# The scale of the first quarter's x goes out to memory and back by GpSimd's queue

## The chip, the cores and the metric

The kernel runs on one core of a Trainium2 chip. A core has a matrix engine (TensorE, PE in the profile), a vector engine (VectorE, DVE), a scalar engine (ScalarE, ACT), GpSimd (POOL) and a queue engine (SyncE, SP), and 16 DMA engines that move data between the chip's memory and the core's. Each engine works through a list of instructions in order and waits at semaphores. The metric is device time in microseconds (us), the median of several runs.

## The reference

The kernel computes one layer of a hybrid decoder on a sequence of 2048 tokens of width 1024. What matters here is how the layer begins, and one part at its end:

```python
hn = rms_norm(h, pre_mix_norm[i])                       # h * rsqrt(mean(h*h) + EPS) * weight
proj = jnp.einsum('btd,dc->btc', hn, w_in[i])           # one projection for all mixers
...
g_dec = -jnp.exp(gdn_a_log[i]) * jax.nn.softplus(a_gdn + gdn_dt_bias[i])
...                                                     # DeltaNet and HGRN2 mixers, output projection, MLP
e = rms_norm(jnp.einsum('bte,ed->btd', p[i], w_ple_proj[i]), ple_norm[i])
gate = jax.nn.sigmoid(jnp.einsum('btd,de->bte', h, w_ple_gate[i]))
h = h + e * gate
```

The first line needs one number for each token, the scale rsqrt(mean(h*h) + EPS). The embedding e depends on p alone, so the kernel can compute it at any time.

## The kernel before, in words

The tokens are worked on in four quarters of 512 (NQ = 4, QT = 512), and all large tiles hold features on the 128 partitions and tokens along the row. Every 32-bit matmul is made of three matmuls of a high and a low part, so each operand tile is first split: ScalarE writes the rounded part (L160), VectorE subtracts it from the original (L161). These two lines serve all weights and inputs.

The kernel starts with a prologue (L349 to L394). It loads the embedding inputs (praw, raw_plea), x with tokens on the partitions (xs, four tokens a partition), x with features on the partitions (xraw) and constants, and computes the embedding tiles (q, d) of the first two quarters while x is made ready.

- The scale: ScalarE squares xs and sums along the row (L375), VectorE adds EPS (L376), GpSimd raises to the power -1/2 (L156, 128x4 numbers). The result ss stands four to a partition, but the tiles of x need it along the row and on every partition. So `spread` stores it to memory (L230, tensor rd_x, 2 KB) and `spread_load` loads it back with each partition reading the whole row (L235, tile rsb_x, 256 KB). VectorE then scales the eight tiles of xraw (L202), and each is split to xt.
- An embedding tile: six matmuls into one of two PSUM banks (L187, tile mme), then ScalarE copies it out (L297, tile e), squares it (L223, tile sq_e, of which there is one, or L220 for the first of a quarter), VectorE adds the square up (L224), and the copy is stored (L299, ed<-e). The square frees the bank for the next tile but one. Six copies e can be in flight.

After the prologue come the projections (from L1009 on): for each of 33 weight blocks of a quarter, 24 matmuls (L1021), first the block of decays (mm_ab), then those of the heads. The loads of the weights (L446), their splits and the stores of the split weights (L176, cache) are requested two or three blocks ahead; the weights of the first two blocks (raw_ab, and raw for the next) are requested at the start of this part. The decays' numbers run through ScalarE and VectorE (L460 to L470), and a short group of matmuls (L480, ps_gb) waits for them in TensorE's order.

The order on TensorE is fixed as the program is traced. On SP the requests of the prologue keep their order among themselves, and so do those of the projections, but the two sequences are merged. This merge, and the order on ScalarE, VectorE and GpSimd, is chosen by a scheduler when the kernel is built, by its own idea of when each input will be there. Once built, the order of each engine is fixed.

The functions that the edit touches:

Of the kernel before, what the change touches and what calls it, by code (L numbers as in the profile page):

```python
# [20 lines left out]
P = 128  # L21
# [3 lines left out]
QT = 512  # L25
NQ = T // QT
NC = QT // P
# [57 lines left out]
def trunk(ctx, tc, x, xT, pT, vecs, w_in, w_ab, gdn_a_log, gdn_dt_bias, w_out, w_up, w_down,  # L85
          w_ple, w_gate, consts, out):
    nc = tc.nc
    V, S, G, PE = nc.vector, nc.scalar, nc.gpsimd, nc.tensor
# [32 lines left out]
    def col(r):  # L121
        return cols[:, r : r + 1]
# [7 lines left out]
    def vectors():  # L130

        ps = bank("ps_rows", pp)
        PE.transpose(ps[:, :N_ROWS], rows, ident[:N_ROWS, :N_ROWS])
        V.tensor_copy(cols, ps[:, :N_ROWS])
        V.tensor_scalar(ple_w, cols[:, R_PLE : R_PLE + KD], 0.5, None, ALU.mult)
        V.tensor_tensor(lb, lg, lg, ALU.subtract)
        S.activation(lb, lb, AF.Exp)
        V.reciprocal(lb1, lb)
        V.tensor_tensor(lb, lb, lb1, ALU.mult)
        V.tensor_tensor(lb, lb, lb, ALU.subtract)  # L140
        V.tensor_scalar(ha, lb, -0.5, 0.5, ALU.mult, ALU.add)
        V.tensor_scalar(hna, ha, -1.0, None, ALU.mult)
        V.tensor_tensor(hb, lb, ha, ALU.add)
        S.activation(nexpa, dec[:, 0:1], AF.Exp)
        V.tensor_scalar(nexpa, nexpa, -1.0, None, ALU.mult)
# [9 lines left out]
    def rsqrt(v):  # L155
        G.tensor_tensor(v, v, mhalf, ALU.pow)  # L156
# [39 lines left out]
    def operand(pool, src, name, scale=None, rsb=None, raw=None, stage=None):  # L196

        if raw is None:
            raw = stage.tile([P, QT], F32, tag="ld", name=f"raw_{name}", bufs=2)
            nc.sync.dma_start(raw, src)  # L200
        if scale is not None:
            V.scalar_tensor_tensor(raw, raw, scale, rsb, ALU.mult, ALU.mult)  # L202
        t = pool.tile([P, 2, QT], F32R, tag="ring", name=name)
        split(t, V, raw)
        return t
# [18 lines left out]
            eng.tensor_tensor(acc, acc, sq, ALU.add)  # L224
        return acc

    def spread(m, name):

        rd = dr.tile([1, QT], F32, name=f"rd_{name}")
        nc.sync.dma_start(rd.rearrange("o (p n) -> (o p) n", n=NC), m)  # L230
        return rd

    def spread_load(rd, name, pool=None, tag="rsb", bufs=2):
        rsb = (pool or st).tile([P, QT], F32, tag=tag, name=f"rsb_{name}", bufs=bufs)
        nc.sync.dma_start(rsb, rd.broadcast_to([P, QT]))  # L235
        return rsb

    def row_norm(acc, scale, eps, name):
# [6 lines left out]
    def tok(q):  # L245
        return slice(q * QT, (q + 1) * QT)
# [30 lines left out]
    def stage_ple(i, name):  # L277

        raw = wp.tile([P, KD, P], F32, tag="raw", name=f"raw_{name}", bufs=2)
        nc.sync.dma_start(raw.rearrange("p (d k) n -> p d k n", k=2),  # L280
                          w_ple[4 * i : 4 * i + 4].rearrange("d p k n -> p d k n"))

        def ready(eng):
            w = wp.tile([P, 2, KD, P], F32R, tag="whl", name=f"w_{name}")
            for half in range(2):
                sl = slice(half * KD // 2, (half + 1) * KD // 2)
                split(w[:, :, sl], eng, raw[:, sl])
            return w

        return ready  # L290

    def embed_tile(q, d, w, pt, accs, pool, bufs):

        ps = bank(f"mme_{q}_{d}")
        project(ps, w[:, :, 2 * (d % 4) : 2 * (d % 4) + 2], pt)
        e = pool.tile([P, QT], F32, tag="ld", name=f"e{q}_{d}", bufs=bufs)
        S.activation(e, ps, AF.Copy)  # L297
        accs[q] = squares(accs[q], ps, d, f"e{q}")
        return lambda: nc.sync.dma_start(ed[q][d], e)  # L299
# [4 lines left out]
    x_r, xts, accs = {}, {0: []}, {0: None, 1: None}  # L304
# [44 lines left out]
    with ExitStack() as ectx:  # L349
        es = ectx.enter_context(tc.tile_pool(name="es", bufs=1))  # L350
        with tc.manual_schedule(engines={mybir.EngineType.SP}):
            ple0 = stage_ple(0, "plea0")
            praw = [es.tile([P, 2, QT], F32, name=f"praw{q}") for q in range(2)]
            nc.sync.dma_start(praw[0], pT[:, tok(0)].rearrange("(k p) t -> p k t", p=P))
            rows4 = x[tok(0), :].rearrange("(p c) d -> p c d", c=NC)
            xs = es.tile([P, NC, D], F32, name="xs")
            for c in range(0, NC, 2):
                nc.sync.dma_start(xs[:, c : c + 2], rows4[:, c : c + 2])
            nc.sync.dma_start(ident, consts[:, C_IDENT])
            nc.sync.dma_start(rows, vecs)  # L360
            nc.sync.dma_start(dec[:, 0:1], gdn_a_log.rearrange("o h -> h o"))
            nc.sync.dma_start(dec[:, 1:2], gdn_dt_bias.rearrange("o h -> h o"))
            nc.sync.dma_start(praw[1], pT[:, tok(1)].rearrange("(k p) t -> p k t", p=P))
            ple1 = stage_ple(1, "plea1")
            xraw = es.tile([P, KD, QT], F32, name="xraw")
            for k in range(0, KD, 2):
                nc.sync.dma_start(xraw[:, k : k + 2],
                                  xT[k * P : (k + 2) * P, tok(0)].rearrange("(k p) t -> p k t", p=P))
            nc.sync.dma_start(cst[:, C_NEG:], consts[:, C_NEG:])

            ple = [ple0(V), None]
            pts = [[operand(ra, None, f"pT{q}_{k}", raw=praw[q][:, k]) for k in range(2)] for q in range(1)]
            ss = sm.tile([P, NC], F32, tag="ss", name="ss_x0")
            for c in range(NC):
                S.activation(xs[:, c], xs[:, c], AF.Square, accum_out=ss[:, c : c + 1])  # L375
            V.tensor_scalar(ss, ss, 1.0 / D, EPS, ALU.mult, ALU.add)  # L376
            rsqrt(ss)
            stores = []
            for d in range(4):
                stores.append(embed_tile(0, d, ple[0], pts[0], accs, es, 6))  # L380
                if d == 1:
                    vectors()
            pts.append([operand(ra, None, f"pT1_{k}", raw=praw[1][:, k]) for k in range(2)])
            ple[1] = ple1(V)
            x_r[0] = spread(ss, "x0")
            rsb = spread_load(x_r[0], "x0")
            for d, q in [(d, 1) for d in range(4)] + [(d, q) for d in range(4, KD) for q in range(2)]:
                stores.append(embed_tile(q, d, ple[d // 4], pts[q], accs, es, 6))
                stores.pop(0)()
                if len(xts[0]) < KD:  # L390
                    k = len(xts[0])
                    xts[0].append(operand(ra, None, f"xt0_{k}", col(R_PREMIX + k), rsb, raw=xraw[:, k]))
            for f in stores:
                f()  # L394


    with mixers as mctx:
# [23 lines left out]
        def x_scale(q):  # L421
            ss2 = sm.tile([P, 2, NC], F32, tag="ss2", name=f"ss2_x{q}")
            rows4 = x[tok(q), :].rearrange("(p c) d -> p c d", c=NC)
            halves, loaded = [(c, a) for c in range(NC) for a in range(2)], []
            for i in range(len(halves) + 1):
                if i < len(halves):
                    c, a = halves[i]
                    t = m2.tile([P, QT], F32, tag="ld", name=f"xs{q}_{c}_{a}", bufs=2)
                    nc.sync.dma_start(t, rows4[:, c, a * QT : (a + 1) * QT])
                    loaded.append(t)  # L430
                if i:
                    c, a = halves[i - 1]
                    t = loaded.pop(0)
                    S.activation(t, t, AF.Square, accum_out=ss2[:, a, c : c + 1])
                yield
            ss = sm.tile([P, NC], F32, tag="ss", name=f"ss_x{q}")
            V.tensor_tensor(ss, ss2[:, 0, :], ss2[:, 1, :], ALU.add)
            V.tensor_scalar(ss, ss, 1.0 / D, EPS, ALU.mult, ALU.add)
            rsqrt(ss)
            yield  # L440
            x_r[q] = spread(ss, f"x{q}")
# [492 lines left out]
        def load_x(q):  # L934

            rsb = spread_load(x_r[q], f"x{q}", m2, "rsx", 1)
            raws = {}

# [737 lines left out]
    rsb = {q: spread_load(ple_r[q], f"pg{q}", None, "acc", 3) for q in (0, 1)}  # L1676
    es, puts = {(q, 0): embedded(q, 0, rsb[q]) for q in (0, 1)}, []
    for half in range(2):
# [4 lines left out]
        for d in range(KD):  # L1683
# [4 lines left out]
            if d + 1 == KD and half == 0:  # L1688
                rsb = {q: spread_load(ple_r[q], f"pg{q}", None, "acc", 3) for q in (2, 3)}
# [65 lines left out]
```

## Time and profile before

| | us |
|---|---|
| median of 3 runs | 2751.11 |
| lowest and highest | 2746.49, 2752.93 |
| the profiled execution | 2749.54 |
| its span in the profile | 2747.7 |

| engine | busy, share of the span |
|---|---|
| TensorE matmuls | 97% |
| VectorE | 74% |
| ScalarE | 54% |
| GpSimd | 4% |

In a row of the timeline stand the start, the duration, the engine, the line, the operation, the tiles it writes and reads, their shapes, and in brackets how long the engine had stood idle before it and what ended this. SPq is SP's queue at the issue of a DMA. A row of the chain of waits has start, duration and what the time went to.

### The profile page before, as it was taken

The page shows a single profiled execution, that of the slowest core. Times are in us where ns is not written, and L with a number is a line of the kernel's source. Part 1 is how long each engine was busy: PE and PEld are TensorE (multiplying, and loading weights), DVE is VectorE, ACT ScalarE, POOL GpSimd, SP SyncE. Part 2 cuts the span into 40 slices and gives each one's busy share as a digit, 9 for nine tenths or more (in the row PEclk, how much of TensorE's full clock was granted, in tenths as well). Part 3 has the DMA queues.
Part 4 walks back from the last instruction along what each step waited for, and adds up shares of the span by engine and source line. Part 5 has one row for each costly group of instructions (what it writes and reads, how often), then busy time and mean ns, then how long its engine had stood idle before and what let it go on. Part 6 is the DMA issues. An engine that isn't in the chain of part 4 may idle for free.

```text
span 2747.7 us, 38450 instructions
## 1 busy us (share of the span) xinstructions
PE 2663.1 (97%) x12745; PEld 2214.6 (81%) x12745; DVE 2044.8 (74%) x4244; ACT 1472.7 (54%) x2944; POOL 104.1 (4%) x104
## 2 busy tenths in 40 slices
PE   7999999999999999899899999999999999999999
PEld 5788788878888888777688888888888888888887
DVE  6788877777777777677798867867787765567776
ACT  6665555455546444666555645555455545465421
POOL 0000000000000000000000000001000000001000
PEclk9999999999999999999999999999999999999999
DMA  7776776666766665787466547667463446677664
GB/s 264 258 251 218 233 249 233 218 213 229 247 207 207 218 212 156 253 303 247 163 228 208 192 160 254 205 212 232 161 225 136 165 154 217 192 253 238 222 210 135
DMA packets 268742, 589.24 MB, mean 214 GB/s; under 512 B 55658, under 2 KB 60232, under 8 KB 249344
## 3 DMA queue, kind: packets, MB, share of 16 engines
q1 hardware_dynamic: 268544, 586.79, 64.4%
q8 instruction: 101, 1.65, 0.3%
q14 instruction: 97, 0.79, 0.1%
HBM read 419.75 MB, written 166.92 MB: 214 GB/s over the span
## 4 chain that ended last, share of the span: by engine, by line
PE 58%; DVE 9%; DMA 6%; issue 5%; ACT 2%; POOL 1%; SPq 0%; DVEq 0%; POOLq 0%; ACTq 0%
PE u L1091 21%; PE d L1091 21%; PE mmg L1091 6%; PE mm L1021 6%; DVE pr_g L659 1%; DMA ud_g<-u_g 1%; DMA sys_g<-ud_g 1%; PE mmo L1091 1%; DVE xs_g L662 1%; DMA raw_out<-in_w_out_dram 1%; DMA rd_g<-m_g 1%; DVE xs_g L664 1%; DMA rsb_g<-rd_g 1%; DVE raw_xt L944 0%; DVE xt L161 0%
## 5 line engine op out<-in xcount | busy, mean ns | idle before, releaser
L1021 PE MATMUL mm<-xt,w 128*128 128x512 f32 x3072 | 770.8, 399 | 3.7 <-DVE acc_vg L503 2.0
L1021 PEld LDWEIGHTS mm<-xt,w 128*128 128x128 f32 x3072 | 559.9, 189 | 110.9 <-DVE acc_vg L503 2.5
L1091 PE MATMUL d<-db,da 128*128 128x512 f32 x2688 | 610.5, 389 | 0.2 <-DVE db L214 0.2
L1091 PE MATMUL u<-t,wu 128*128 128x512 f32 x2604 | 592.1, 389 | 3.4 <-ACT wu L160 3.4
L1091 PEld LDWEIGHTS d<-db,da 128*128 128x128 f32 x2688 | 504.5, 188 | 105.5 <-DVE db L214 0.6
L1091 PEld LDWEIGHTS u<-t,wu 128*128 128x128 f32 x2604 | 488.5, 188 | 106.3 <-ACT wu L160 4.2
L214 DVE TENSOR_TENSOR db<-db 128x512 fp32r<-128x512 f32 x224 | 160.7, 717 | 71.8 <-ACT db L213 71.3
L1420 DVE TENSOR_TENSOR u<-u,u 128x512 f32<-128x512 f32 x224 | 150.6, 683 | 62.7 <-PE u L1091 60.6
L213 ACT ACTIVATE db<-db 128x512 fp32r<-128x512 f32 x224 | 141.1, 630 | 79.6 <-DMA db<-hid 76.2
L1091 PE MATMUL mmo<-mixT,w_out 128*128 128x512 f32 x720 | 168.7, 395 | 10.3 <-DVE w_out L161 7.3
L1091 PE MATMUL mmg<-h2T,wg 128*128 128x512 f32 (+1 forms) x792 | 174.8, 383 | 0.0
L1461 ACT ACTIVATE u<-u 128x512 f32<-128x512 f32 x128 | 81.0, 632 | 167.2 <-DVE u L1420 166.8
L1091 PEld LDWEIGHTS mmo<-mixT,w_out 128*128 128x128 f32 x720 | 136.8, 191 | 41.3 <-DVE w_out L161 9.0
L1091 PEld LDWEIGHTS mmg<-h2T,wg 128*128 128x128 f32 x792 | 145.5, 188 | 29.1
L161 DVE TENSOR_TENSOR da<-da 128x512 fp32r<-128x512 f32 x128 | 92.6, 723 | 82.0 <-ACT da L160 81.7
L160 ACT ACTIVATE da<-da 128x512 fp32r<-128x512 f32 x128 | 80.6, 629 | 122.5 <-DMA da<-sumd 105.0
L160 ACT ACTIVATE wu<-a 128x512 fp32r<-128x512 f32 x124 | 74.0, 623 | 48.2 <-DMA a<-in_w_up_dram 46.7
L659 DVE TENSOR_TENSOR pr_g<-xs_g,sys_g 128x16 f32<-128x16 f32 (+14 forms) x240 | 93.9, 391 | 5.3
L224 POOL TENSOR_TENSOR acc_y<-acc_y,sq_y 128x512 f32<-128x512 f32 x28 | 38.3, 1369 | 1370.0 <-ACT sq_y L223 1369.2
L161 DVE TENSOR_TENSOR wu<-a,wu 128x512 fp32r<-128x512 f32 x124 | 84.9, 688 | 4.5 <-ACT wu L160 4.5
L1462 ACT ACTIVATE u<-u 128x512 f32<-128x512 f32 x128 | 80.8, 632 | 3.7
L161 DVE TENSOR_TENSOR da<-dr,da 128x512 fp32r<-128x512 f32 x96 | 66.4, 691 | 20.0 <-ACT da L160 17.6
(378 smaller groups left out, 3808.1 us busy)
## 6 DMA issues: line engine op xcount, KB each, us to landing
w<-cache_in SPq DMA_DIRECT2D x96, 1024.0 KB
db<-hid SPq DMA_DIRECT2D x224, 256.0 KB
cache_in<-w SPq DMA_DIRECT2D x32, 1024.0 KB
hid<-u SPq DMA_DIRECT2D x128, 256.0 KB
da<-sumd SPq DMA_DIRECT2D x128, 256.0 KB
a<-in_w_up_dram SPq DMA_DIRECT2D x124, 256.0 KB
hid<-ht SPq DMA_DIRECT2D x96, 256.0 KB
dr<-in_w_down_dram SPq DMA_DIRECT2D x96, 256.0 KB
```

The lines of the kernel that those rows point to most:

```text
L160: S.activation(t[:, 0], raw, AF.Copy)
L161: eng.tensor_tensor(t[:, 1], raw, t[:, 0], ALU.subtract)
L213: S.activation(t[:, 0], plain(t), AF.Copy)
L214: V.tensor_tensor(t[:, 1], plain(t), t[:, 0], ALU.subtract)
L224: eng.tensor_tensor(acc, acc, sq, ALU.add)
L659: V.tensor_tensor(pr[:, :, :, 0:i], xs[:, None, :, 0:i].broadcast_to([P, 2, GC, i]), sys[:, 0:i, i : i + 2].rearrange("p j two -> p two j" ...
L662: V.tensor_reduce(xs[:, :, i : i + 2].rearrange("p g two -> p two g"), pr[:, :, :, 0 : i + 1], AX.X, ALU.add)
L1021: PE.matmul(ps, *terms[i], start=i == 0, stop=i == nt - 1)
L1091: PE.matmul(ps, a, b, start=start, stop=stop)
L1420: V.tensor_tensor(c[new], c[old], ps, ALU.add)
L1461: S.activation(c[k], c[k], AF.Relu)
L1462: S.activation(c[k], c[k], AF.Square)
```

## The change

The store of the scale and its load, for the first quarter alone, are issued by GpSimd instead of SP. The other three quarters, and all other users of the two functions, keep SP.

```diff
-    def spread(m, name):
+    def spread(m, name, queue=nc.sync):
 
         rd = dr.tile([1, QT], F32, name=f"rd_{name}")
-        nc.sync.dma_start(rd.rearrange("o (p n) -> (o p) n", n=NC), m)
+        queue.dma_start(rd.rearrange("o (p n) -> (o p) n", n=NC), m)
         return rd
 
-    def spread_load(rd, name, pool=None, tag="rsb", bufs=2):
+    def spread_load(rd, name, pool=None, tag="rsb", bufs=2, queue=nc.sync):
         rsb = (pool or st).tile([P, QT], F32, tag=tag, name=f"rsb_{name}", bufs=bufs)
-        nc.sync.dma_start(rsb, rd.broadcast_to([P, QT]))
+        queue.dma_start(rsb, rd.broadcast_to([P, QT]))
         return rsb
...
-            x_r[0] = spread(ss, "x0")
-            rsb = spread_load(x_r[0], "x0")
+            x_r[0] = spread(ss, "x0", G)
+            rsb = spread_load(x_r[0], "x0", queue=G)
```

The scheduler answers with other orders in the first 100 us or so; behind that, all engines keep theirs. The parts of the built order that move (ScalarE, from the square of embedding tile (1,1) to that of (0,4); SP, from the constants on):

```
ScalarE before: sq(1,1) w_ab w xt0 e(1,2) xt1 sq(1,2) xt2 e(1,3) sq(1,3) xt3 e(0,4) sq(0,4)
ScalarE after:  sq(1,1) xt0 xt1 xt2 xt3 xt4 e(1,2) sq(1,2) e(1,3) xt5 sq(1,3) e(0,4) sq(0,4)
SP before: rd_x, raw_ab, raw, rsb_x, seven stores ed, raw, ...
SP after:  eight stores ed, raw_ab, one store ed, raw, three stores ed, raw, ...
```

Behind the prologue, ScalarE's first convolution step of the first head (L499) moves ahead of the decays' exponential (L466), a weight split moves ahead of L460, and on VectorE one weight split moves behind six small operations (L827).

## The prediction

> **What bounds the kernel now.** I read the page's first parts for the whole, then the windows, the waits of TensorE and the timeline of the first 64 us, because the edit lies there.
>
> ```profile
> span 2747.7 us, 38450 instructions
> PE 2663.1 (97%) x12745; PEld 2214.6 (81%) x12745; DVE 2044.8 (74%) x4244; ACT 1472.7 (54%) x2944; POOL 104.1 (4%) x104
> ```
> TensorE is the bound of the run as a whole. What the edit can move is the time at which its steady work starts.
>
> ```profile
> 24.50:30.30 5.80, 0.35 (x3) 0.02 (x1) 4.20 (x6) 3.84 (x7) 0.00 (x0) 0.97 1.01 390
> 30.30:45.10 14.80, 13.81 (x48) 9.61 (x48) 13.36 (x21) 11.89 (x23) 0.00 (x0) 0.90 0.66 230
> ```
> These are windows (length; busy time of PE, PEld, DVE, ACT, POOL; clock; DMA share; GB/s). From 24.5 to 30.3 TensorE stands, and the DMA engines are full. The timeline says why:
>
> ```profile
> 16.03 1.02 POOL L156 TENSOR_TENSOR ss_x<-ss_x,mhalf 128x4 f32<-128x4 f32 x1 [15.59 <-DVE ss_x L376]
> 17.08 0.35 SPq L230 DMA_DIRECT2D rd_x<-ss_x  x1
> 17.53 0.39 SPq L446 DMA_DIRECT2D raw_ab<-in_w_ab_dram  x1
> 21.66 0.33 SPq L446 DMA_DIRECT2D raw<-in_w_in_dram  x1
> 23.62 0.33 SPq L235 DMA_DIRECT2D rsb_x<-rd_x  x1
> 24.03 1.06 ACT L160 ACTIVATE w_ab<-raw_ab 128x1024 fp32r<-128x1024 f32 x1 [0.91 <-DMA raw_ab<-in_w_ab_dram]
> 26.23 1.06 ACT L160 ACTIVATE w<-raw 128x1024 fp32r<-128x1024 f32 x1 [1.14 <-DMA raw<-in_w_in_dram]
> 27.32 2.08 DVE L202 SCALAR_TENSOR_TENSOR xraw<-xraw,cols,rsb_x 128x512 f32<-128x512 f32 x3 [0.97 <-DMA rsb_x<-rd_x]
> 28.11 0.63 ACT L160 ACTIVATE xt<-xraw 128x512 fp32r<-128x512 f32 x1 [0.82 <-DVE xraw L202]
> 28.64 0.58 ACT L297 ACTIVATE e<-mme 128x512 f32<-128x512 f32 x1
> 29.64 0.59 ACT L223 ACTIVATE sq_e<-mme 128x512 f32<-128x512 f32 x1
> 30.28 0.80 PE L187 MATMUL mme<-pT,w_plea 128*128 128x512 f32 x1 [5.45 <-ACT sq_e L223]
> 35.51 1.29 DVE L161 TENSOR_TENSOR xt<-xraw,xt 128x512 fp32r<-128x512 f32 x2
> 45.12 5.76 PE L1021 MATMUL mm_ab<-xt,w_ab 128*128 128x512 f32 x24 [0.34 <-ACT sq_e L223]
> ```
> The scale is ready at 17.05 and usable on all partitions at 27.32; call this second moment R. ScalarE runs its list in order. It waits for two weight tiles, then for R, and only behind them evicts the embedding tile that frees a PSUM bank for TensorE. So the stall of 5.45 us hangs on R and on what stands in ScalarE's list ahead of that eviction. The projections start at 45.12, which is R + 17.80.
>
> **The change part by part.** *The transfers.* Two issues (0.35 and 0.33 us) leave SP's queue for GpSimd's. No queue work of GpSimd is in the way: its next instruction, the memset at L674, has 33.8 us of idle time before it, so the load that waits for the store's landing holds up nothing there. R becomes 17.05 plus a store and a load in a row. No row shows a transfer issued by GpSimd, so I bound the pair by SP's.
>
> ```profile
> 61.41 0.26 SPq L474 DMA_DIRECT2D gd<-gb  x1
> 62.82 0.32 SPq L568 DMA_DIRECT2D gf_g<-gd  x1
> 596.60 3.77 DMA rd_g<-m_g
> 600.39 4.88 DMA rsb_g<-rd_g
> 655.36 8.32 DMA rd_g<-m_g
> 663.69 4.75 DMA rsb_g<-rd_g
> ```
> Below: the small store of gd was followed by its dependent load after 1.41 us, and today's broadcast took 3.70 (23.62 to 27.32); R = 17.05 + 1.41 + 3.70 = 22.2. Above: the slowest pair of the same two shapes in the chain of waits, 8.32 + 4.75, gives R = 30.1. The nearest is the other pair of these shapes, 3.77 + 4.88 = 8.65, R = 25.7: the DMA engines are loaded in both places.
>
> What GpSimd itself adds is unknown. It is not free of VectorE:
>
> ```profile
> 61.52 2.60 POOL L156 TENSOR_TENSOR m_e<-m_e,mhalf 128x4 f32<-128x4 f32 x1 [10.36 <-DVE m_e L270]
> 62.02 1.20 DVE L161 TENSOR_TENSOR w<-raw,w 128x1024 fp32r<-128x1024 f32 x1
> 75.12 1.01 POOL L156 TENSOR_TENSOR rk_g<-rk_g,mhalf 128x4 f32<-128x4 f32 x1 [11.00 <-DVE m_e L270]
> ```
> The same small operation took 2.60 beside a VectorE subtraction, and 1.01 elsewhere: 1.6 us at stake, nothing at best. VectorE subtracts nearly without a break until 21.6, which is when the store would be made, so I take the 1.6 once: R = 27.3. That is where it is today; the way out of SP's queue is then worth nothing.
>
> [...]
>
> *The order on ScalarE and VectorE.* The scheduler takes the scale to come early, and the weights late, and reorders. On ScalarE, behind the square of embedding tile (1,1), stood: w_ab, w, xt0, e(1,2), xt1, sq(1,2). Now stand there xt0, xt1, xt2, xt3, xt4, e(1,2), sq(1,2); w_ab comes after sq(0,5), w after e(0,6). VectorE has two scalings of xraw, one accumulation, two subtractions, then three scalings. By the rows a scaling takes 0.75 and starts 0.65 to 0.7 after the last (three in 2.08), a subtraction 0.69 and starts 0.6 later (two in 1.29). So the fifth scaling starts at R + 2x0.65 + 3x0.59 + 2x0.65 = R + 4.37 and ends, with hand-over, at R + 5.16; then xt4 (next start 0.53 later), e (0.50 later) and the square with hand-over (0.64): TensorE resumes at R + 6.8, where it was R + 2.96. This is the cost: four more tiles of the scale-dependent work stand ahead of the eviction.
>
> From there to the projections I carried both orders forward by the same durations (eviction and square 0.60, split 0.63, accumulation and subtraction 0.69, weight split 1.06 on ScalarE and 1.23 on VectorE, six matmuls 1.62; one square at a time; two PSUM banks). For the order before this gives 44.94 where 45.12 was measured. For the changed order it gives R + 21.26; with the same error, R + 21.4. Three splits are gone from that stretch and two weight splits have come in, so it stays near 14.5 us. The shift of the projections' start is therefore s = R + 21.4 - 45.1 = R - 23.7, and not below -1.8 (what is left when R no longer binds).
>
> *The queue of SP.* SP no longer waits for the scale, so the embedding stores go out from 14 us on, and the loads of w_ab and of the first w move behind eight and nine of those stores, which wait for ScalarE. By the same working w_ab's load is issued at R + 7.7 and needed at R + 13.3. The first w's load, from 21.66 to 26.23, took 4.6 with the engines full: covered by 1 us. w_ab's own 6.5 (17.53 to 24.03) would cost 0.9. I take nothing.
>
> *A second reordering, behind the first projections.*
>
> ```profile
> 50.97 0.68 ACT L460 ACTIVATE sp<-mm_ab,dec 4x512 f32<-4x512 f32 x1 [3.46 <-PE mm_ab L1021]
> 51.17 7.42 PE L1021 MATMUL mm<-xt,w 128*128 128x512 f32 x32
> 55.58 1.28 ACT L466 ACT_TABLE_LOAD   x1
> 56.87 0.63 ACT L466 ACTIVATE se<-se 4x512 f32<-4x512 f32 x1
> 57.53 0.69 ACT L499 ACTIVATE acc_kg<-mm,cols 128x512 f32<-128x512 f32 x1
> 57.54 0.68 DVE L467 SCALAR_TENSOR_TENSOR sp<-sp,se 4x512 f32<-4x512 f32 x1 [0.20 <-ACT se L466]
> 63.57 0.25 PE L480 MATMUL ps_gb<-cst,gbb 36*128 36x36 f32 x1 [2.83 <-DVE gbb L477]
> ```
> The decays' exponential (L466) now stands behind the first convolution step (L499), which needs all 24 matmuls of that projection. These end 23/32 of 7.42 plus 0.4 after 51.17, at 56.9. Then 0.6, the table load 1.28 and the exponential 0.63: VectorE gets it at 59.4, not at 57.54. TensorE is already waiting at the end of this chain (2.83 us at 63.57), so 1.9 us come on top of s. The weight split w_8 also moves ahead of L460 and costs 1.6 there, hidden under VectorE's memsets, which hold L464 until 54.2; without that cover the two would add up only in part.
>
> *Later.* One weight split on VectorE moves behind six small operations near 92 us: its end moves from 93.5 to about 94.4, and the load behind it left at 94.09, so about 0.3. Behind that the order is the same to the end.
>
> **Sum.** s + 1.9 + 0.3 with R = 27.3: 3.6 + 1.9 + 0.3 = +5.8 us. The profiled execution took 2749.5 (its span and 1.8 around it), 1.6 under the median of 2751.1; its sum is 2755.3, and against the median 2756.9. What a measurement of this kernel can tell from no change is about 0.2%, 5.5 us; the runs before spread over 6.4.
>
> **Rivals.** *The pair is quick (same).* With a queue of its own the store does not stand behind the loads of SP's queue, where it took from 17.08 to 23.62 to land. By the lower rows R = 22.2 to 24.6, the sum +0.7 to +3.1, say 2753. It decides below R = 27.0. For it: 128 x 16 bytes is little. Against: the same store took 8.32 to land in one place. [...]
>
> *The pair is slow (slower still).* Upper rows plus the 1.6: R = 30.1 + 1.6 = 31.7, sum 8.0 + 2.2 = +10.2, 2761. Anything that the first DMA of GpSimd has to set up falls here too.
>
> *Faster.* SP, free from 14 us, and an early scale could dissolve the whole stall before 30.28. That takes R below 18 by the working above, because the evictions stand behind five splits; then 5.45 us go, and the total is 5.5 or better only if the exponential's 1.9 hide as well: 2745.6. Against: R - 6.8 us of list work remains ahead of the bank, and no pair of rows is shorter than 5.1 us.
>
> *Absorbed (same).* The early loss could be taken back where TensorE waits later. Against: those waits hang on work that TensorE's own order triggers, so they move along. 2751.
>
> **How the numbers follow.** Forecast (R 26 to 30): 0.45. Quick pair: 0.31. Slow pair: 0.11. Absorbed: 0.07. Faster: 0.06. The forecast's lower edge, R 26 to 27, lies within 0.2%: I count 0.04 of it as same. So slower 0.52, same 0.42, faster 0.06. The range reaches from 2750 (the quick pair's lower bound, less the runs' error of 1 us) to 2763 (the slow pair and as much on top).
>
> **What would show it.** A GpSimd row for L230 just after 17.05, and L202 on VectorE at R. TensorE resuming 6.8 us behind R; mm_ab at R + 21.4; L467 14.3 us behind mm_ab's start, where it was 12.4; ps_gb's wait grown by 1.9. I am wrong if R lies outside 22 to 32, if TensorE's resumption does not follow R, or if the shift at 64 us is not the shift at the end.

## The result, and the profile after

| | before | after |
|---|---|---|
| median, run side by side | 2749.55 (2744.50 to 2755.09, 20 runs) | 2753.09 (2747.98 to 2759.67, 20 runs) |
| ratio after / before | | 1.0016, 95% interval 1.0009 to 1.0022 |
| the profiled execution, and its span | 2749.54, 2747.7 | 2749.35, 2747.6 |

The change costs 0.16% (0.0016 x 2750 = 4.4 us; the two medians lie 3.5 apart): slower, by less than the 0.2% that the prediction called the limit of a measurement. The two profiled executions have the same length by chance, so no conclusion can be drawn from their spans; what the profile is good for here is the first 75 us. The timeline of the changed kernel (columns as before: start, duration, engine, line, operation, tiles, shapes, idle time and what ended it):

```profile
17.37 0.73 POOL L230 DMA_DIRECT2D rd_x<-ss_x  x1 [0.30 <-POOL ss_x L156]
...
24.85 0.56 POOL L235 DMA_DIRECT2D rsb_x<-rd_x  x1 [6.75 <-DMA rd_x<-ss_x]
28.80 1.42 DVE L202 SCALAR_TENSOR_TENSOR xraw<-xraw,cols,rsb_x 128x512 f32<-128x512 f32 x2 [7.16 <-DMA rsb_x<-rd_x]
29.58 1.29 ACT L160 ACTIVATE xt<-xraw 128x512 fp32r<-128x512 f32 x2 [6.46 <-DVE xraw L202]
...
32.71 1.96 ACT L160 ACTIVATE xt<-xraw 128x512 fp32r<-128x512 f32 x3 [1.84 <-DVE xraw L202]
...
34.58 0.58 ACT L297 ACTIVATE e<-mme 128x512 f32<-128x512 f32 x1
35.05 0.59 ACT L223 ACTIVATE sq_e<-mme 128x512 f32<-128x512 f32 x1
...
35.69 9.41 PE L187 MATMUL mme<-pT,w_plea 128*128 128x512 f32 x30 [10.83 <-ACT sq_e L223]
...
50.93 5.75 PE L1021 MATMUL mm_ab<-xt,w_ab 128*128 128x512 f32 x24
...
62.60 0.69 ACT L499 ACTIVATE acc_kg<-mm,cols 128x512 f32<-128x512 f32 x1 [0.74 <-PE mm L1021]
...
64.60 0.63 ACT L466 ACTIVATE se<-se 4x512 f32<-4x512 f32 x1
...
65.26 0.68 DVE L467 SCALAR_TENSOR_TENSOR sp<-sp,se 4x512 f32<-4x512 f32 x1 [1.62 <-ACT se L466]
...
71.11 0.32 PE L480 MATMUL ps_gb<-cst,gbb 36*128 36x36 f32 x1 [2.68 <-DVE gbb L477]
```

Both transfers are issued by GpSimd. R, the moment at which the scale is usable, is 28.80 (before 27.32). ScalarE then makes five splits of xt (2 + 3) ahead of the eviction of embedding tile (1,2) at 34.58, and TensorE's stall has grown from 5.45 to 10.83 us. The projections start at 50.93 (before 45.12), the decays' logarithm (L466; called the exponential up to here) comes behind L499, and the last wait for ps_gb ends at 71.11 (before 63.57): 7.5 us late.

Since single executions differ, both kernels were profiled twice more (runs e1, e5, e10, e11 below). The means of three:

| | before | after | difference |
|---|---|---|---|
| R | 27.32, 28.29, 26.87: 27.49 | 28.80, 28.72, 28.53: 28.68 | +1.2 |
| from R to the start of mm_ab | 17.80, 18.59, 17.80: 18.06 | 22.13, 21.53, 21.93: 21.86 | +3.8 |
| from mm_ab to the start of L467 | 12.42, 12.71, 12.13: 12.42 | 14.33, 14.35, 14.32: 14.33 | +1.9 |
| end of the last wait for ps_gb | 63.57, 65.62, 62.83: 64.01 | 71.11, 70.44, 70.62: 70.72 | +6.7 |

So there are three losses in a row, 1.2 from the transfers, 3.8 from the order behind them and 1.9 from the second reordering, 6.9 in all; the last wait for ps_gb ends 6.7 us later than before.

### The profile page after: what moved, and what is told of

Read it like the earlier page. It is cut to its first block, busy times and chain, and to the rows that moved or that the text cites. A ratio compares the mean times of both kernels' runs of the same rounds, so it can differ in the third digit from the quotient of the medians.

```text
span 2747.6 us, 38453 instructions
## 1 busy us (share of the span) xinstructions
PE 2660.8 (97%) x12745; PEld 2214.5 (81%) x12745; DVE 2044.5 (74%) x4244; ACT 1471.3 (54%) x2944; POOL 103.4 (4%) x106
## 4 chain that ended last, share of the span: by engine, by line
PE 67%; DVE 13%; DMA 8%; issue 6%; ACT 4%; POOL 1%; SPq 1%; POOLq 0%; DVEq 0%; ACTq 0%
PE d L1091 22%; PE u L1091 21%; PE mm L1021 12%; PE mmg L1091 6%; DVE pr_g L659 2%; DMA ud_g<-u_g 2%; DVE xs_g L662 1%; DMA sys_g<-ud_g 1%; DVE xs_g L664 1%; PE mmo L1091 1%; PE at_h L814 1%; PE mme L187 1%; DMA rd_g<-m_g 1%; DMA mixT<-mixd 1%; DMA rsb_g<-rd_g 1%
## 5 line engine op out<-in xcount | busy, mean ns | idle before, releaser
L160 ACT ACTIVATE wu<-a 128x512 fp32r<-128x512 f32 x124 | 73.9, 622 | 46.5 <-DMA a<-in_w_up_dram 45.0
L161 DVE TENSOR_TENSOR da<-dr,da 128x512 fp32r<-128x512 f32 x96 | 66.2, 690 | 21.4 <-ACT da L160 19.3
```

The costliest lines, as they stand in the source:

```text
L160: S.activation(t[:, 0], raw, AF.Copy)
L161: eng.tensor_tensor(t[:, 1], raw, t[:, 0], ALU.subtract)
```

## Experiments

In the diffs, `tc.issue_after(i)` makes the scheduler place what follows behind instruction i; `.ins` is the handle of an instruction. Where lines of code move, the line numbers in a profile move too. All runs in one table: times in us, "back" is the moment at which TensorE resumes after the stall near 25 us, "ps_gb" the end of its last wait, the ratio is against the kernel before, run on the same chip.

| run | R | back | mm_ab | mm_ab - R | ps_gb | ratio (95%) |
|---|---|---|---|---|---|---|
| before, mean of 3 | 27.5 | 30.5 | 45.6 | 18.1 | 64.0 | |
| e5, e11: before again | 28.29, 26.87 | 31.24, 29.83 | 46.88, 44.67 | 18.6, 17.8 | 65.6, 62.8 | 0.9996 (0.9985 to 1.0008), 1.0000 (0.9990 to 1.0010) |
| e1, e10: after again | 28.72, 28.53 | 35.62, 35.42 | 50.25, 50.46 | 21.5, 21.9 | 70.4, 70.6 | 1.0017 (1.0008 to 1.0027), 1.0032 (1.0020 to 1.0044) |
| e2: after's order, SP's queue | 27.76 | 34.65 | 49.86 | 22.1 | 67.5 | 1.0003 (0.9994 to 1.0012) |
| e6: store alone on GpSimd | 26.25 | 29.21 | 45.19 | 18.9 | 64.9 | 0.9997 (0.9985 to 1.0009) |
| e7: load alone on GpSimd | 28.44 | 25.48 | 46.49 | 18.1 | 62.3 | 0.9990 (0.9979 to 1.0001) |
| e8: less ahead of the store | 26.89 | 32.47 | 49.88 | 23.0 | 67.6 | 1.0002 (0.9989 to 1.0015) |
| e9: ScalarE's list put back | 28.60 | 31.70 | 50.64 | 22.0 | 70.8 | 1.0024 (1.0013 to 1.0034) |
| e4: evictions first, SP's queue | | 29.01 | 47.01 | | 66.5 | 1.0014 (1.0004 to 1.0023) |
| e3: logarithm ahead again | 28.64 | 35.53 | 50.45 | 21.8 | 69.5 | 1.0012 (1.0001 to 1.0023) |
| e12: before, decays' chain first | 27.63 | 30.59 | 45.72 | 18.1 | 61.0 | 0.9984 (0.9974 to 0.9995) |

**Is it the order or the queue?** The theory is that the order costs. The rival is that the transfers cost more on GpSimd's queue. Run e2 takes the order without the queue.

```diff
 for d, q in ...:                       # both transfers on SP's queue
+    if (q, d) == (1, 2):
+        for k in range(5):
+            with tc.issue_after(seen[1, 1][0].ins):     # the square of (1,1)
+                xts[0].append(operand(...))
+        seen["xt"] = list(last_split)
-    stores.append(embed_tile(q, d, ...))
+    with tc.issue_after(seen.get("xt", mark)[0].ins):
+        stores.append(embed_tile(q, d, ...))
...
-    split_work(0)
+    split_behind(0, seen[0, 5])
-    split_work(1)
+    split_behind(1, seen[0, 6])
```

> The kernel before, both transfers on SP's queue, with ScalarE's list put by hand into the order of the changed kernel up to the projections: five splits of xt ahead of the eviction of embedding tile (1,2), w_ab's split behind the square of (0,5). The logarithm stays ahead of L499. If the cost is the order: the scale is usable at 27.3 as before, TensorE resumes 6.8 us behind that (34.1) instead of 3.0, mm_ab starts at 48.7 to 49.4 instead of 45.1, ps_gb moves by the same 3.6 to 4.3, and with half of it taken back later the time is 1.5 to 3 us over the kernel before. If the cost is the queue: mm_ab starts within 0.7 us of 45.1 and the time is that of the kernel before.

Its timeline:

```profile
23.67 0.33 SPq L239 DMA_DIRECT2D rsb_x<-rd_x  x1
...
27.76 2.08 DVE L204 SCALAR_TENSOR_TENSOR xraw<-xraw,cols,rsb_x 128x512 f32<-128x512 f32 x3 [4.63 <-DMA rsb_x<-rd_x]
...
34.65 8.78 PE L189 MATMUL mme<-pT,w_plea 128*128 128x512 f32 x30 [10.52 <-ACT sq_e L227]
...
49.86 5.74 PE L1036 MATMUL mm_ab<-xt,w_ab 128*128 128x512 f32 x24
```

With SP's queue TensorE resumes 6.9 us behind R, and mm_ab starts 22.1 behind R, as in the changed kernel (6.9 and 21.5 to 22.1). So the order makes this loss without the queue (mm_ab at 49.86, expected 48.7 to 49.4). The time was expected 1.5 to 3 us over the kernel before and came 0.8 over (-1.7 to +2.5 by its interval). The scheduler had given this kernel another list behind mm_ab too: TensorE does not wait at ps_gb at all, and there the loss is 3.5 instead of 6.7 us. So e2 shows the loss at mm_ab, and its time can't be told from that of the kernel before.

Runs e6 and e7 take one transfer each.

```diff
-            rsb = spread_load(x_r[0], "x0", queue=G)      # e6, from the changed kernel
+            rsb = spread_load(x_r[0], "x0")
...
-            x_r[0] = spread(ss, "x0", G)                  # e7, from the changed kernel
+            x_r[0] = spread(ss, "x0")
```

> The changed kernel with the store alone on GpSimd's queue; the load goes back to SP's. In the changed kernel the store took 7.2 to 7.5 us from its issue to its landing, and the load 3.9. If the store is what made the scale late (its packets ran only when SP's backlog had drained), the scale is usable at 28.3 to 29.3 us here too. If the load on GpSimd's queue is what made it late, it is usable at about 27.3. ScalarE's list is a third one here (the second eviction comes ahead of the second split), so TensorE resumes 3 to 5 us behind the scale, and mm_ab follows it by 18 to 21 us: 46.5 to 50.

> The changed kernel with the load alone on GpSimd's queue; the store stays on SP's. If the store makes the scale late, it is usable within 0.5 us of 27.5 here (store landed near 23.6, load 3.9 behind it); if the load does, at 28.3 or later. ScalarE's list here has the evictions and squares of (1,2) and (1,3) ahead of the first split of xt, so TensorE does not wait for the scale at first: it resumes before 28 us. If the list ahead of the eviction is what cost the changed kernel its 10.8 us stall, that stall is gone and mm_ab starts at 43 to 47; if splits that come late hold it up, near 48 as in the kernel that evicts first on SP's queue.

The timeline of e6:

```profile
17.28 0.72 POOL L230 DMA_DIRECT2D rd_x<-ss_x  x1 [0.30 <-POOL ss_x L156]
...
22.27 0.35 SPq L235 DMA_DIRECT2D rsb_x<-rd_x  x1
...
26.25 2.08 DVE L202 SCALAR_TENSOR_TENSOR xraw<-xraw,cols,rsb_x 128x512 f32<-128x512 f32 x3 [2.51 <-DMA rsb_x<-rd_x]
...
29.21 5.98 PE L187 MATMUL mme<-pT,w_plea 128*128 128x512 f32 x18 [4.46 <-ACT sq_e L223]
```

And of e7:

```profile
23.73 0.71 POOL L235 DMA_DIRECT2D rsb_x<-rd_x  x1 [7.00 <-DMA rd_x<-ss_x]
...
25.48 3.04 PE L187 MATMUL mme<-pT,w_plea 128*128 128x512 f32 x12 [0.98 <-ACT sq_e L223]
...
28.44 2.08 DVE L202 SCALAR_TENSOR_TENSOR xraw<-xraw,cols,rsb_x 128x512 f32<-128x512 f32 x3 [2.29 <-DMA rsb_x<-rd_x]
...
33.67 10.81 PE L187 MATMUL mme<-pT,w_plea 128*128 128x512 f32 x30 [5.16 <-ACT sq_e L223]
```

Neither has five splits ahead of the eviction, and neither loses the 3.8 us: mm_ab starts 18.9 and 18.1 behind R. Neither is measurably slower than the kernel before. The expectation on R failed for e6: the store from GpSimd was quick (5.0 us from its issue to that of the load) and R was 26.25, the lowest of all. In e7 the load took 4.7 us from its issue to R (before: 3.7, 4.7 and 3.7). R was 28.44, where the expectation put a slow load (28.3 or later); but one profile of the kernel before has R at 28.29, so this run alone does not decide it.

**What does the store wait for?** In the changed kernel it took 7.5, 5.9 and 6.2 us from its issue to that of the load. The DMA view of the changed kernel between 14 and 34 us (packets, MB, share of 16 engines; then issue, KB each, us to landing):

```profile
q1 hardware_dynamic: 2155, 4.35, 63.9%
q0 software_dynamic: 112, 0.26, 5.0%
...
rsb_x<-rd_x POOLq DMA_DIRECT2D x1, 256.0 KB, 3.9
rd_x<-ss_x POOLq DMA_DIRECT2D x1, 2.0 KB, 7.2
```

GpSimd's queue is q0, SP's is q1. Run e8 takes away a part of what SP's queue has in front of the DMA engines at that time.

```diff
-            nc.sync.dma_start(cst[:, C_NEG:], consts[:, C_NEG:])     # 640 KB, ahead of the loop
...
-                stores.pop(0)()
+                stores.pop(-1 if (q, d) == (1, 0) else 0)()
...
+            nc.sync.dma_start(cst[:, C_NEG:], consts[:, C_NEG:])     # behind the loop
             for f in stores:
```

> The changed kernel with 640 KB of constants loaded behind the embedding loop instead of ahead of it, and the first embedding stores held until the loop's last tiles of that step, so that SP's queue has that much less in front of the DMA engines when GpSimd issues its store at 17.4. If the store's packets wait until SP's backlog is through, the store lands 1.5 us or more earlier (by 23.3 or before, where it was 24.0 to 24.8 and 22.7), the load behind it likewise, and the scale is usable at 27 or earlier. If GpSimd takes that time itself to make the descriptors beside VectorE, the store lands where it did, 5.9 to 7.5 us behind its issue, and the scale stays at 28.7.

Its timeline:

```profile
16.53 0.73 POOL L230 DMA_DIRECT2D rd_x<-ss_x  x1 [0.30 <-POOL ss_x L156]
...
21.71 0.56 POOL L235 DMA_DIRECT2D rsb_x<-rd_x  x1 [4.46 <-DMA rd_x<-ss_x]
26.89 1.41 DVE L202 SCALAR_TENSOR_TENSOR xraw<-xraw,cols,rsb_x 128x512 f32<-128x512 f32 x2 [6.11 <-DMA rsb_x<-rd_x]
...
44.62 1.06 ACT L160 ACTIVATE w<-raw 128x1024 fp32r<-128x1024 f32 x1 [1.20 <-DMA raw<-in_w_in_dram]
...
46.22 1.65 PE L187 MATMUL mme<-pT,w_plea 128*128 128x512 f32 x6 [1.57 <-ACT sq_e L223]
```

The store landed by 21.7 and R is 26.89, as expected if the backlog holds the store. mm_ab does not follow: three splits instead of five stand ahead of the eviction, but later ScalarE waits 1.20 us for the first w, TensorE 1.57 for the square behind it, and mm_ab starts 23.0 us behind R.

From the packet records of the traces (in the time of the timelines), for every run with the store on GpSimd's queue: when its issue ended, when its first packet ran, and when the rate of SP's queue first fell under 200 GB/s (in steps of 0.25 us), which is when its backlog was through.

```
                 issue ended   first packet   SP's backlog through
e8 less ahead       17.26          19.00            19.50
e6 store only       18.00          20.65            21.25
e1 after            17.56          20.86            22.50
e3                  17.84          21.22            22.50
e10 after           17.88          21.26            22.75
e9                  18.11          21.55            23.00
after               18.10          21.57            23.00
```

The order of the second column is that of the third, and the first packet comes 0.5 to 1.6 us ahead of the end of the backlog, but 1.7 to 3.5 us behind the issue. In e8, with the same work beside it on VectorE, it ran 1.7 us behind the issue. So in these seven runs the store waited for most of the backlog on SP's queue, though it was on another queue; what GpSimd needs by itself after the issue is 1.7 us at most, by e8. In the three profiles of before, on SP's own queue, the store's first packet ran 3.1 to 3.3 us behind its issue, no later than in the changed kernel (3.3 to 3.5). From its last packet to its landing another 0.5 to 2.5 us pass in the seven runs; why this varies stays open.

With both transfers on GpSimd SP no longer stops at the scale and puts five or six embedding stores of 256 KB in front of the DMA engines by 22.5 us. They take the place of the two weight loads of 512 KB that stood there before, and the backlog lasts at least as long as it did (through at 22.50, 22.50 and 22.25 in the three profiles of before). In e6 SP stops for the load, neither stores nor weights go out before 22.71, and the backlog ends earliest of the runs that load all constants there.

The load fared the same. In the three profiles of the changed kernel it was issued at 24.85, 22.76 and 23.33, but its first packet ran at 26.28, 25.61 and 25.38, near the time at which the embedding stores were through (SP's rate fell under 200 GB/s again at 26.00, 26.25 and 26.00), and R came at 28.80, 28.72 and 28.53. So a store that landed 2 us earlier made R hardly earlier. Before the change the load stood ahead of these stores in SP's list. In e8, where SP's queue was through at 24.00, the load's first packet ran at 24.28; no run moved these stores alone.

**Is it ScalarE's list alone?** Run e9 keeps both transfers on GpSimd and puts back only how many splits stand ahead of the eviction.

```diff
+        with tc.issue_after(hold[0].ins) if hold else ExitStack():
             S.activation(t[:, 0], raw, AF.Copy)                # split, L160
...
+                    hold[:] = mark if k > 1 else []            # mark: the square of this tile
                     xts[0].append(operand(ra, None, f"xt0_{k}", ...))
+                    hold[:] = []
```

> The changed kernel, both transfers on GpSimd's queue, with one thing of ScalarE's list put back: the split of xt2 and those behind it each wait for the square of their own embedding tile, so that only two splits, not five, stand ahead of the eviction of (1,2). If that list is what the change cost, the scale is still usable at 28.3 to 29.0, TensorE resumes 3.3 to 4.2 us behind it instead of 6.9, and mm_ab starts 18 to 19.5 us behind it (46.5 to 48), where the changed kernel had 50.3 and 50.9; the time is 2 to 4 us under the changed kernel. If the queue costs by itself, mm_ab stays at 49.5 or later.

Its timeline:

```profile
31.70 2.93 PE L190 MATMUL mme<-pT,w_plea 128*128 128x512 f32 x6 [6.86 <-ACT sq_e L227]
31.73 4.06 DVE L205 SCALAR_TENSOR_TENSOR xraw<-xraw,cols,rsb_x 128x512 f32<-128x512 f32 x6
...
35.71 0.69 DVE L228 TENSOR_TENSOR acc_e<-acc_e,sq_e 128x512 f32<-128x512 f32 x1
...
36.43 0.60 ACT L227 ACTIVATE sq_e<-mme 128x512 f32<-128x512 f32 x1 [2.80 <-DVE acc_e L228]
...
37.08 7.72 PE L190 MATMUL mme<-pT,w_plea 128*128 128x512 f32 x24 [2.45 <-ACT sq_e L227]
```

TensorE does resume 3.1 us behind R. But VectorE's list was left to the scheduler, which put six scalings (4.06 us) ahead of the accumulation L228. There is one tile sq_e, so ScalarE's next square waits 2.80 us for that accumulation, and TensorE 2.45 for the square. The gain was lost again by 37 us, mm_ab starts 22.0 behind R, and the time (1.0024) is among the changed kernel's (1.0016 to 1.0032). My expectation, 46.5 to 48, was wrong: the loss hangs on the lists of both engines, and one of them put back alone moves the wait to the other.

Run e4 tried the opposite on SP's queue: the scalings and splits of x traced four embedding tiles later, so that evictions come first.

```diff
-                if len(xts[0]) < KD:
-                    xts[0].append(operand(...))
+                seen[q, d] = list(mark)
+                for _ in range({(0, 4): 2, (1, 4): 2, (0, 5): 1, (1, 5): 1, (0, 7): 1, (1, 7): 1}.get((q, d), 0)):
+                    xt_behind(seen[q, d])       # under issue_after that tile's square and accumulation
...
-            split_work(0)
+            split_behind(0, seen[0, 5])
```

> The kernel before, transfers on SP's queue, with the work that waits for the scale traced four embedding tiles later, so that ScalarE evicts (1,2), (1,3), (0,4) and (1,4) ahead of the first split of xt. The scale is usable at 27 to 28. If the stall of 5.45 us came from what stands ahead of the eviction in ScalarE's list, it shrinks to under 1.5 us, mm_ab starts near 42 (3 us earlier), and the time is 1.5 to 3 us under the kernel before. Rival: the splits that come later hold up the projections instead, mm_ab starts at 45 or later and the time does not fall.

Its timeline:

```profile
27.87 0.60 ACT L299 ACTIVATE e<-mme 128x512 f32<-128x512 f32 x1 [4.76 <-DMA ed<-e]
...
29.01 8.16 PE L187 MATMUL mme<-pT,w_plea 128*128 128x512 f32 x24 [4.20 <-ACT sq_e L225]
...
33.70 1.41 DVE L202 SCALAR_TENSOR_TENSOR xraw<-xraw,cols,rsb_x 128x512 f32<-128x512 f32 x2
```

The stall went from 5.45 to 4.20 only, since behind the list stands a second reason: the eviction waits for an embedding store (six copies e can be in flight), and on SP's queue those stores stand behind the load of the scale. In e7, where SP does not wait for the load, the stall at this place was 0.98, but TensorE then waited 5.16 us at 33.67, behind the splits. In e4 the late scalings (from 33.70) then hold up the projections, as the rival said: mm_ab at 47.01. Whether evictions first would gain with both transfers on GpSimd, where the stores are free, was not tried.

**The second reordering.** Run e3 puts the logarithm back ahead of L499 in the changed kernel.

```diff
-            S.activation(se, se, AF.Ln, bias=1.0)
+            logs.append(S.activation(se, se, AF.Ln, bias=1.0))
...
+                    if s == SPT - 1 and j == 1:
+                        with tc.issue_after(logs[0].ins):
+                            then(ps, q, h, g, b)
...
```

> The changed kernel with one step put back: the logarithm of the decays (L466) ahead of the first convolution step (L499). mm_ab starts as in the changed kernel (50.9). The first wait of ps_gb falls from 3.3 to about 1.4 us and ps_gb starts near 69.2 instead of 71.1. If the 1.9 us of this reordering reach the end, the time is 1.5 to 2.5 over the kernel before, some 1.9 under the changed kernel; if they are among what is taken back before 290 us, it is that of the changed kernel, 3 to 5 over the kernel before.

Its timeline:

```profile
62.84 0.63 ACT L468 ACTIVATE se<-se 4x512 f32<-4x512 f32 x1
...
63.49 0.69 ACT L501 ACTIVATE acc_kg<-mm,cols 128x512 f32<-128x512 f32 x1
63.50 0.68 DVE L469 SCALAR_TENSOR_TENSOR sp<-sp,se 4x512 f32<-4x512 f32 x1 [0.20 <-ACT se L468]
...
69.51 0.32 PE L482 MATMUL ps_gb<-cst,gbb 36*128 36x36 f32 x1 [2.74 <-DVE gbb L479]
```

VectorE has the logarithm 13.05 us behind mm_ab's start, where it was 14.33; ps_gb stands 19.1 behind mm_ab's start instead of 20.2. So 1.1 of the 1.9 us came back at ps_gb. The time, against the changed kernel run beside it, is 2752.56 against 2754.80; the intervals of the two ratios overlap, so what of it reaches the end can't be told from the times.

Run e12 asks the same of the kernel before: how much does the decays' chain cost there? It moves the chain on VectorE ahead of the convolution's taps, on SP's queue.

```diff
+            def turn_back():                                   # in decays
+                back = mt(f"gbb_{q}", "gbb", 1, (36, QT // 2))
+                backs.append(V.tensor_copy(...))               # L477
+                return back
+
+            back = turn_back() if q == 0 else None
             yield
...
+                with tc.issue_after(backs[0].ins) if name == "kg0_0" else ExitStack():
                     V.scalar_tensor_tensor(acc[:, d:], ...)    # the taps, L503
```

> The kernel before, transfers on SP's queue, with one thing moved on VectorE: the rest of the decays' chain (L468, L470 and the copy L477) ahead of the taps of the first convolution, so that ps_gb no longer waits behind them. mm_ab starts where it did (45 to 47). If the chain is what holds TensorE there, the waits of ps_gb fall from 4.2 to about 1.5 us, ps_gb starts 2.5 to 3 us earlier against mm_ab, and the time is 2 to 4 us under the kernel before. If the convolution's taps are as urgent, TensorE waits for them a little later and the time stays within 1 us of the kernel before.

The timeline of the kernel before at this place:

```profile
60.03 1.35 DVE L470 TENSOR_TENSOR_SCAN gb<-one,sp 4x128 f32<-4x128 f32 x4
...
61.36 0.73 DVE L503 SCALAR_TENSOR_TENSOR acc_kg<-mm,cols,acc_kg 128x511 f32<-128x511 f32 x1
...
62.02 1.20 DVE L161 TENSOR_TENSOR w<-raw,w 128x1024 fp32r<-128x1024 f32 x1
...
63.24 0.27 DVE L477 COPY gbb<-gb 36x256 f32<-36x256 f32 x1
```

And of e12:

```profile
59.27 1.36 DVE L472 TENSOR_TENSOR_SCAN gb<-one,sp 4x128 f32<-4x128 f32 x4
...
60.66 0.28 DVE L478 COPY gbb<-gb 36x256 f32<-36x256 f32 x1
...
61.00 0.25 PE L488 MATMUL ps_gb<-cst,gbb 36*128 36x36 f32 x1 [1.02 <-DVE gbb L478]
```

A tap and a weight split stood between the scan and the copy; without them ps_gb is ready 15.3 us behind mm_ab's start instead of 18.2 to 18.7, and the waits fall from 4.3 (1.45 + 2.83) to 1.0. The time is 0.9984 (0.9974 to 0.9995), 4.4 us under the kernel before: the one version here that is faster than both kernels beyond its interval, by an edit that has nothing to do with the queue.

**Does the early loss reach the end?** The two kernels were run again, twice each. Run e1 first:

> The changed kernel once more. What it tells apart is where the early loss goes. Theory one, 'half stays': the projections start about 5.8 us later than before (near 50.9 us) and ps_gb about 7.5 us later, some 4 us of it are taken back between 60 and 290 us, and 3.2 to 3.9 us stand from there to the end; the time is 3 to 5 us over the kernel before. Theory two, 'nothing stays': the shift falls to about 0 between 690 and 870 us, as it did in the first profiled pair, and the time is within 1 us of the kernel before.

> The kernel before once more, for a second profile of it and for what two runs of one program differ by. In the first profiles the changed kernel, run twice, was 7.5 and 8.1 us later at ps_gb, 5.6 and 7.7 at 110 to 140 us, 3.9 and 6.9 at 260 to 300 us, and 0.8 and 2.2 at 800 to 900 us. If all of that decline is the changed kernel taking time back, the second profile of the kernel before agrees with the first within 0.5 us up to 900 us, and the decline shows against it too. If part of it is the first profile losing time of its own, the second one runs 1.5 to 3 us ahead of the first by 870 us, and the two of the changed kernel then stay 3 to 5 us behind it. The times differ by less than 0.1%.

> The changed kernel a third time, for the size of the shift along the run. From the two profiles of each kernel so far, means: 6.4 us at 66 to 75, 5.5 at 110 to 140, 3.6 at 300 to 400, 3.1 at 800 to 900, 4.6 at the end. If about half of the early loss is taken back between 75 and 400 us, the mean of three against three lies at 5.5 to 7.5 us at ps_gb and at 2.5 to 4.5 at 300 to 400. If that decline was chance, the two means differ by less than 1.

> The kernel before a third time, for the same means. The scale is usable between 27.0 and 28.5, mm_ab starts 17.6 to 18.8 us behind it, and the half-speed stretches of TensorE's clock are one of 3.4 to 6.8 us behind the stall near 25 us and one of the same size behind the wait for ps_gb.

Run e1 had theory one's time (4.7 us over) and not its course: 1.2 us were taken back between 75 and 300 us, not 4. Run e11 had R a little under the expected 27.0, mm_ab 17.8 behind it, and stretches at half speed of 3.4 and 6.8 us. How late the same TensorE instructions are after the change, mean of three profiles against mean of three, from the timelines:

```
stretch, us      45-56  66-75  110-140  220-260  300-400  600-700  800-900  end
after - before    5.0    7.2     6.6      5.9      4.9      5.1      4.9    5.8
```

The first pair of profiles had fallen to nothing by 870 us; that was the executions and not the change: e5 and e11 run 3.2 and 4.4 us ahead of the first profile of before at 800 to 900 us, and the changed kernel's three lie 0.7 to 4.8 us behind it. About a third of the loss, 2.3 of 7.2 us, is taken back by 400 us, less than the half that I had expected (4.9 is left there, not 2.5 to 4.5); the rest stays. At the end single executions of the same kernel lie up to 10 us apart, so its 5.8 is rough. The times say the same: three ratios, 1.0016, 1.0017 and 1.0032, weighted by their intervals 1.0019, or 5.2 us. Over the ten kernels of the table (both kernels as means) the time follows the moment of ps_gb: a straight line has 0.95 us at the end for each us there (correlation 0.93; e2 and e8, 3.5 us late there and 0.8 and 0.5 at the end, lie farthest below it, e4 above). With the start of mm_ab the correlation is 0.72 only: e2 and e8 start mm_ab 4.3 us late, nearly as late as the changed kernel (5.0), and e8 has both transfers on GpSimd, but neither is measurably slower than the kernel before. So what the first reordering alone costs at the end is not shown.

One place where time is taken back shows in all six profiles. The windows from 274 to 298 us (length; busy time of PE, PEld, DVE, ACT, POOL; clock; DMA share; GB/s), before:

```profile
274.00:298.00 24.00, 20.82 (x109) 17.57 (x108) 19.14 (x58) 8.30 (x17) 0.00 (x0) 0.93 0.75 252
```

and after:

```profile
274.00:298.00 24.00, 20.89 (x115) 17.47 (x115) 18.68 (x58) 7.54 (x17) 0.00 (x0) 1.00 0.76 228
```

The granted clock was 0.93 in all three profiles of before and 1.00 in all three of after. Just ahead of it TensorE waits for r_g: 2.7, 2.6 and 2.9 us before, 2.2, 2.2 and 2.1 after. Together that is up to 0.5 + 1.7 us; the table falls by 1.0 there. Why the wait is shorter after the change was not tried.

## Why the prediction was right or wrong

- **Direction and size.** The sum was +5.8 us, the likeliest case "slower" by just over 0.2%. Measured were +4.4 in the first comparison (3.5 between the medians), and 5.2 over all three. The time forecast, 2756.9, is 3.8 over the 2753.09 measured; 1.6 of that is that the kernel before itself ran at 2749.55 this time and not at 2751.11.
- **R: the term that was mis-sized.** Predicted 8.65 for the pair and 1.6 for GpSimd, R = 27.3, no later than before. Measured 28.5 to 28.8, 1.2 later than the mean of before. The pair took 11.4 to 11.9 us from the store's issue. What was mis-sized is the wait for the DMA engines: SP's backlog held the store (its first packet ran at 19.00 in e8, 20.65 in e6 and 21.57 in the changed kernel, with the backlog through at 19.50, 21.25 and 23.00), and it lasted as long as before (22.25 to 22.50 there), because the embedding stores that SP now issues from 14 us on (the prediction names them) filled it up. So the store took about what it did (issue to the load's issue 6.5 in the mean, before 6.4), and the 1.2 are nearly all in the load, which now has embedding stores in front of it: 4.0, 6.0 and 5.2 us, where SP's took 3.7, 4.7 and 3.7. Whether GpSimd lost 1.6 us to VectorE can't be told; by e8 its own time is 1.7 at most.
- **The quick pair (0.31)** failed for the same reason: a queue of its own did not let the store pass (first packet 1.7 to 3.5 us behind its issue, against 3.1 to 3.3 on SP's queue). R lay above 24.6 in every run.
- **The order: right.** TensorE was to resume R + 6.8, and did at R + 6.9 in each of the three; mm_ab was to start at R + 21.4, and did at R + 21.5 to 22.1. The order alone did it on SP's queue too (e2). What the 0.5 over is stays open; TensorE's clock, which the prediction left out (below), differs little here (half of the busy time in the first half-speed stretch is 1.5 to 2.6 us before, 1.7 to 2.3 after).
- **SP's queue: right to take nothing.** w_ab's load left at R + 7.8 (predicted 7.7) and nothing waited for it.
- **The second reordering: right in place and size** at L467: 14.33 behind mm_ab's start, predicted 14.3. The first wait of ps_gb grew from 1.4 to 3.3. The weight split of 0.3 near 92 us left no mark on TensorE: the shift does not grow there.
- **"Later": wrong in part.** The prediction said that later waits move along with TensorE, and made it a condition that the shift at 64 us is the shift at the end. About a third was taken back, by 400 us.
- So +1.2 was missing and 2.3 given back was missing, and the sum came out near by luck: the errors offset each other.
- **The rival "faster"** named the true cost: evictions behind the splits. No run dissolved the stall: e7, in which SP does not wait for the load and evictions come first, has 0.98 us here and 5.16 later, where before had 5.45. Its mm_ab - R is as before, ps_gb 1.7 us earlier, and the time 0.9990 with 1.0 inside its interval.

## What to carry to other kernels

Moving a transfer to another queue is also an order to the scheduler: compare the built lists of all engines first, because here, by the end of the waits for ps_gb, the new order cost 5.7 us and the transfers themselves 1.2. A queue of its own did not take a store of 2 KB past the backlog that another queue had put in front of the same DMA engines (first packet 0.5 to 1.6 us ahead of the backlog's end), and the queue that was freed filled the gap with the next transfers in its list (five or six of 256 KB by 22.5 us). Before a list is put back by hand, look for every ring of buffers that ties two engines' lists together; putting back one list moved the wait to the other (2.80 us on ScalarE in e9).

## What the runs showed of the hardware

In the traces TensorE's granted clock fell from 1.00 to 0.50 in a long stall and stayed there for a while after it: in the first profile of the kernel before it fell at 29.94, TensorE resumed at 30.28, and the clock rose again at 33.35; in that of the changed kernel these were 30.13, 35.69 and 40.37. Matmuls of 512 columns started 0.43 us apart at half speed instead of 0.23. From the clock records of the traces, the stretches at half speed last 3.4, 6.8, 10.2 or 13.7 us. At the first stall it is one of 3.4 or 6.8 us in the kernel before (5.0 to 6.5 us idle), and one of 10.2 in all three profiles of the changed kernel (10.8 to 11.3 idle); at the waits for ps_gb, 3.4 to 6.8 before, 6.8 to 10.2 after, and none in e12. The half of TensorE's busy time in them, an upper bound of what they cost, is 3.2, 5.1 and 4.1 us in the first 100 us before, and 4.2, 5.0 and 5.6 after; in e12 it is 2.1. In these two first profiles the changes of the clock, up to its last fall, lie whole multiples of 3.41 us apart (17.07, 3.41, 30.72 and 218.45 in that of before). Near 286 us the waits of 2.6 to 2.9 us before the change were followed by such a stretch of 3.4, and those of 2.1 to 2.2 after it were not. But the length of the wait did not decide it: near there a wait of 2.8 in e12 was followed by none, and one of 2.0 in e8 was. In the traces the fall went with the share of a window of 3.41 us, counted from these changes, in which TensorE was busy. At full speed, in the fourteen traces, each window in which TensorE was busy for less than 0.46 of the time was followed by half speed, and none with more than 0.53 (105 falls in some 11,000 windows). Near 286 us the least busy window had 0.28, 0.24 and 0.16 before and 0.51, 0.57 and 0.46 after, 0.57 in e12 and 0.43 in e8.

So in this kernel, which TensorE bounds, a stall could cost more than its length: by an estimate from these stretches up to 1.7 us for one of 3.4 (its half), which neither a sum of waits nor the busy share shows.
